# A float32 decoder trunk on one core: another engine for the decays' low halves, other ticks for the decay blocks, another queue for the first transfers

## The chip, the core and the metric

The kernel runs on one core of a Trainium2 chip. The core has a matrix engine (TensorE, here PE), a vector engine (VectorE, here DVE), an engine for activations (ScalarE, here ACT), one for general work (GpSimd, here POOL) and a queue of transfers (SyncE, here SP). Each takes its instructions in order, and they wait for one another through semaphores. The metric is the device time of one execution in microseconds (us), as a median of runs.

## What is computed

One inference step of a two-layer decoder trunk over 336 tokens: 256 of a new prompt, 64 of eight running sequences (8 each), 16 meta tokens. A layer is a half-step SwiGLU block, a mixer, and a second half-step SwiGLU block. The mixer joins gated linear attention (GLA) and a depthwise convolution:

```
proj = x @ w_in
q, k, v, g, a_lr, glu, m_a, m_b = split(proj)
loga = log_sigmoid(a_lr @ w_decay_up + b_decay) / 16
b = cumsum(loga, within a chunk)
scores = mask((q * exp(b)) @ (k * exp(-b)).T)
o = scores @ v + (q * exp(b)) @ S
S = exp(b_last) * S + (k * exp(b_last - b)).T @ v
a, ga = split(glu);  u = a * sigmoid(ga)
c = silu(rmsnorm(depthwise_conv(u, 31 taps)))
merged = sigmoid(m_a) * rmsnorm(o) * silu(g) + sigmoid(m_b) * (c @ w_pw)
h = h + merged @ w_out
```

The decays `loga` and their running sums `b` are what the change is about: they must be ready before the attention can start.

## The kernel before

**Products.** Tokens lie along the free axis, channels along the partitions, eight blocks of 128. All products are made to float32 accuracy from pairs of a shorter type: a value is split into a high half (a cast, `wh`, `xh`, `lah`) and a low half (value minus high half, `wl`, `xl`, `lal`), and each product is three matmuls (`mm3`: high x high, high x low, low x high). One k-step of `mm3` at 336 columns is called a tick.

**Weights.** SP loads 512 KB pieces into four raw buffers (`W.load`), ACT casts each (`wh`, L214), and VectorE (L112, the helper through which all VectorE work is recorded) or POOL (L215) subtracts (`wl`). In the mixer it is POOL for most pieces, the decays' place included; in the SwiGLU blocks it is VectorE. `use` of a piece splits up to three pieces further on and loads up to four more.

**The mixer.** PE goes through three `glu` blocks, then the value blocks with the decays' input, then five more `glu` blocks (`pga`, then `pa`, 8 ticks each). A `glu` block on VectorE is a multiplication of `pga`, after which ACT makes the gate, then one of `pa` and three into `u`. Beside it, work is drawn from a list by ticks (`tasks`, filled from the table `at` in the mixer): decay_z multiplies the low-rank input (`pz`, L463 and on), ACT takes exponential and logarithm, decay_min on VectorE finishes `la` for three groups `g` of tokens at ticks 63, 65, 67, and decay_split (L472 to L474) at ticks 66, 70, 74 casts `lah` on ACT and subtracts `lal`. Then decay_prompt(hd) for the four heads (`pb`): four matmuls each, cumulating `lah` and `lal` of groups 0 and 1, and on ACT three exponentials (`qt`, `kt`, `ku`) and one small one (`dec`, L490). decay_tail(0) and decay_tail(2) do the same for group 2, two heads each (`pbt`). `pb` and `pbt` share one tag of two PSUM buffers, so each waits until the one before the last has been read by ACT.

**Fillers.** VectorE also computes the convolution, 31 taps for each of eight blocks of `u`, a tap being a pair of instructions (`acc`, `acs`, L427 to L430). These pairs are drawn by fill(): the program keeps two estimates of time used, for PE and for VectorE (`clock`; VectorE's is added to by every call through `DVE`), and after each tick adds pairs until VectorE's estimate is 1 us ahead of PE's. After the last tap of a block ACT copies `acc` and `acs` back into `u` (L432 to L435) and squares it (L295). The pairs that are left in the last head are drawn at one place, conv_flush.

**The start.** The first two transfers, the norm columns `vec` and blocks 0 and 1 of `h`, are issued from ACT's queue (L851, L852), beside SP's, which issues the first weight pieces, the rest of `h` and more weights. From `h` and `vec` come `xh` and `xl`; the first weight piece is cast in two parts, and the first matmul follows.

Of the kernel before, what the change touches and what calls it, by code (L numbers as in the profile page):

```python
# [9 lines left out]
F32 = mybir.dt.float32  # L10
# [3 lines left out]
ALU = mybir.AluOpType  # L14
# [38 lines left out]
V_DW = 104  # L53
# [64 lines left out]
def trunk_kernel(ctx, tc, wts, x_in, vecs, consts, cumw, masks, wdecay, cache, state,  # L118
                 y_out, sp_out, ss_out, u_out):
    nc = tc.nc  # L120
    PE, ACT, POOL, SP = nc.tensor, nc.scalar, nc.gpsimd, nc.sync
# [5 lines left out]
    DVE = Clocked(nc.vector, dve_time)  # L127
# [13 lines left out]
    h = cst.tile([128, KB, T], F32, name="h")  # L141
# [3 lines left out]
    vec = cst.tile([128, NV], F32, name="vec")  # L145
# [13 lines left out]
    def vcol(base, l, b, n=KB):  # L159
        return vec[:, base + l * n + b:base + l * n + b + 1]  # L160

    def bank(name, tag="mm", bufs=4):
        return psum.tile([128, 512], F32, tag=tag, name=name, bufs=bufs)
# [155 lines left out]
    def emit_x(b, gcol, norm, n=T, add=True):  # L319
        src = h[:, b, 0:n]  # L320
        ACT.activation(xh[:, b, 0:n], src, AF.Identity, scale=gcol)
        DVE.scalar_tensor_tensor(out=xl[:, b, 0:n], in0=src, scalar=gcol, in1=xh[:, b, 0:n].bitcast(F32),
                                 op0=ALU.mult, op1=ALU.subtract)
        if add:
            norm.add(src, n)
# [43 lines left out]
    def mixer(l, norm, next_block):  # L369
# [8 lines left out]
        lah = mp.tile([128, 3, 512], F32R, tag="wg", name="lah")  # L378
        lal = mp.tile([128, 3, 512], F32R, tag="sb", name="lal")
# [15 lines left out]
        la = {}  # L395
# [75 lines left out]

        def decay_split(g):  # L472
            ACT.copy(lah[:, g], la[g])
            POOL.tensor_tensor(out=lal[:, g], in0=la[g], in1=lah[:, g].bitcast(F32), op=ALU.subtract)  # L474

        def cumulate(out, hd, g):
            hs = slice(hd * DK, (hd + 1) * DK)
            m = cum[:, 0:2 * CHUNK] if g < NCH else cum[:, 2 * CHUNK:N_CUM]
            mm(out, lah[:, g, hs], m, True, False)
            mm(out, lal[:, g, hs], m, False, True)  # L480

        def decay_prompt(hd):
            pb = bank("pb", "aux", 2)
            for g in range(NCH):
                cumulate(pb[:, 2 * g * CHUNK:2 * (g + 1) * CHUNK], hd, g)
            v4 = pb.rearrange("p (g x c) -> p g x c", g=NCH, x=2)
            for dst, x, sign in ((qt, 0, 1.0), (kt, 0, -1.0), (ku, 1, 1.0)):
                ACT.activation(dst[:, hd, 0:SEQ].rearrange("p (g c) -> p g c", g=NCH), v4[:, :, x], AF.Exp,
                               scale=sign / TAU)
            ACT.activation(dec[:, hd, 0:2 * NCH], pb[:, CHUNK - 1::CHUNK], AF.Exp, scale=1.0 / TAU)  # L490

        def decay_tail(h0):
            pb = bank("pbt", "aux", 2)
            for e in range(2):
                cumulate(pb[:, 2 * e * TAIL:2 * (e + 1) * TAIL], h0 + e, NCH)
            v4 = pb[:, 0:4 * TAIL].rearrange("p (h x c) -> p h x c", h=2, x=2)
            hh = slice(h0, h0 + 2)
            for dst, x, sign in ((qt, 0, 1.0), (kt, 0, -1.0), (ku, 1, 1.0)):
                ACT.activation(dst[:, hh, SEQ:T], v4[:, :, x], AF.Exp, scale=sign / TAU)
            ACT.activation(dec[:, hh, 2 * NCH:], v4[:, :, 0, LS - 1:NSAMP:LS], AF.Exp, scale=1.0 / TAU)  # L500
# [65 lines left out]
        at = {0: decay_lr, 20: decay_alr, 50: decay_exp, 54: decay_ln, 118: decay_end}  # L566
        for g in range(3):
            at.update({44 + g: lambda g=g: decay_z(g), 63 + 2 * g: lambda g=g: decay_min(g),
                       66 + 4 * g: lambda g=g: decay_split(g)})
        for hd in range(HEADS):  # L570
            at[82 + 5 * hd] = lambda hd=hd: decay_prompt(hd)
        at.update({103: lambda: decay_tail(0), 109: lambda: decay_tail(2)})
        tasks.extend([at.get(k) for k in range(119)])
        v_proj(1)
        v_proj(2)
# [188 lines left out]
        def head_start(hd):  # L764
            st = hs[hd]
            return {0: lambda: (scores(hd, st), spread_q(hd), mask_ku(hd, st)), 1: lambda: prompt_state(hd, st, 0),
                    2: lambda: prompt_state(hd, st, 1)}
# [22 lines left out]
        at = head_start(0)  # L790
# [57 lines left out]
        mx.close()  # L848

    with tc.manual_schedule():  # L850
        ACT.dma_start(vec[:, :V_DW], vecs[:, :V_DW])  # L851
        ACT.dma_start(h[:, 0:2], x_in[:, 0:2])  # L852
        W.load(1)
        SP.dma_start(h[:, 2:5], x_in[:, 2:5])
        SP.dma_start(h[:, 5:KB], x_in[:, 5:KB])
        W.load(W.RAW - 1)
        DVE.memset(eps, EPS)
        DVE.memset(ones_d, 1.0 / D)
        DVE.memset(ones_v, 1.0 / DV)
        ACT.activation(scratch, eps, AF.Square)  # L860
        DVE.memset(one, 1.0)
        for p in probs:
            DVE.memset(p, 0.0)

        def block_to(base, l, n=T):
            nm = Norm()
            return nm, (lambda b: emit_x(b, vcol(base, l, b), nm, n))

        def side_loads(l):
            ACT.dma_start(u, cache[l])  # L870
            if l == 0:
                SP.dma_start(con, consts)
                SP.dma_start(msk, masks)
                SP.dma_start(vec[:, V_DW:], vecs[:, V_DW:])
                zero = tmp.tile([128, KB], F32, tag="zero", name="zero", bufs=1)
                DVE.memset(zero, 0.0)
                for t in (xh, xl):
                    ACT.copy(t[:, :, T:TP], zero.unsqueeze(2).to_broadcast([128, KB, TP - T]))

        norm = Norm()  # L880
        for b in range(KB):
            emit_x(b, vcol(V_F1, 0, b), norm, add=False)
            if b == 1:
                W.split(1)
        W.split(2)
        for b in range(KB):
            norm.add(h[:, b], eng=DVE)
        for l in range(DEPTH):
            n = TY if l == DEPTH - 1 else T
            nxt, to = block_to(V_MIX, l)  # L890
            ffn(norm, to, ready=KB - 1 if l else 2, aside=lambda: side_loads(l))
            norm = nxt
            nxt, to = block_to(V_F2, l, n)
            mixer(l, norm, to)
            norm = nxt
            if l + 1 < DEPTH:
                nxt, to = block_to(V_F1, l + 1)
            else:
                nxt = Norm()
                to = lambda b, nm=nxt: (nm.add if b < KB - 1 else nm.add_last)(h[:, b, 0:TY], TY)  # L900
            ffn(norm, to, n)
            norm = nxt
        r = norm.rstd(ones_d, TY)
        for b in range(KB):
            DVE.scalar_tensor_tensor(out=h[:, b, 0:TY], in0=h[:, b, 0:TY], scalar=vec[:, V_FIN + b:V_FIN + b + 1],
                                     in1=r[:, 0:TY], op0=ALU.mult, op1=ALU.mult)
            SP.dma_start(y_out[:, b], h[:, b, 0:TY])
# [125 lines left out]
```

## Time and profile before

| | us |
|---|---|
| median of 3 runs | 1633.62 (1631.21 to 1634.97) |
| profiled execution | 1631.83 |
| its span | 1629.7 |
| PE busy | 1598.5 (98%) |
| VectorE busy | 1079.7 (66%) |
| ACT busy | 735.9 (45%) |
| POOL busy | 401.8 (25%) |

The span runs from the program's first instruction to its last; the profiled execution's own time is 2.1 us longer. Busy time is the sum of an engine's instructions; PE's overlap and its weight loads run beside its matmuls. Where an engine has an idle time, the profile names the instruction whose semaphore came last. [...]

### The profile page before, as it was taken

How to read it: one execution, taken by the hardware profiler on the slowest of the kernel's cores; microseconds unless marked ns; L12 is line 12 of the kernel's file. 1: busy time of each engine (PE TensorE's matmuls, PEld its weight loads, DVE VectorE, ACT ScalarE, POOL GpSimd, SP SyncE). 2: the span in 40 equal slices, each digit the busy share in tenths (PEclk: the TensorE clock that was granted, in tenths of full speed). 3: DMA queues.
4: the chain of work that ended last, by engine and by line, in shares of the span. 5: the costliest groups of instructions: out<-in, count | busy, mean ns of one | idle time of the engine just before them, and what ended most of it. 6: DMA issues, size and time to landing. Idle time of an engine off the chain costs nothing.

```text
span 1629.7 us, 26967 instructions
## 1 busy us (share of the span) xinstructions
PE 1598.5 (98%) x10516; PEld 1571.6 (96%) x10516; DVE 1079.7 (66%) x2170; ACT 735.9 (45%) x1153; POOL 401.8 (25%) x290
## 2 busy tenths in 40 slices
PE   7999999999999999999999999999999999999997
PEld 7999999999889999999999999999998799999997
DVE  6656545999986566564456654459999766666633
ACT  5433434673546444333343333346645564443432
POOL 0000005676663300000000000066766632000000
PEclk9999999999999999999999999999999999999999
DMA  5554444555544544444446444444555445444352
GB/s 198 196 171 136 133 144 146 164 158 164 162 163 131 166 131 155 142 131 142 151 139 205 151 132 139 154 131 152 178 174 166 155 141 160 150 157 147 120 169 77
DMA packets 77023, 247.78 MB, mean 152 GB/s; under 512 B 8672, under 2 KB 11360, under 8 KB 76640
## 3 DMA queue, kind: packets, MB, share of 16 engines
q1 hardware_dynamic: 75744, 239.76, 46.1%
q10 hardware_dynamic: 1152, 6.31, 1.1%
q8 instruction: 82, 1.34, 0.3%
q14 instruction: 45, 0.37, 0.1%
HBM read 230.33 MB, written 15.71 MB: 151 GB/s over the span
## 4 chain that ended last, share of the span: by engine, by line
PE 88%; DVE 7%; ACT 1%; DMA 1%; POOL 1%; issue 1%; DVEq 0%; ACTq 0%; POOLq 0%
PE pd L134 20%; PE pg L134 20%; PE pu L134 20%; PE pgate L134 9%; PE po L134 4%; PE pw L134 3%; DVE acc L112 3%; PE pv L134 2%; PE pa L134 2%; PE pga L134 2%; PE pk L134 2%; PE pq L134 2%; DVE acs L112 1%; PE upds L134 1%; PE o L134 1%
## 5 line engine op out<-in xcount | busy, mean ns | idle before, releaser
L112 DVE TENSOR_TENSOR wl<-raw,wh 128x1024 fp32r<-128x1024 f32 (+3 forms) x331 | 361.6, 1109 | 244.2 <-ACT wh L214 243.8
L214 ACT CAST wh<-raw 128x1024 fp32r<-128x1024 f32 (+4 forms) x457 | 427.0, 954 | 60.8 <-issue 26.7
L215 POOL TENSOR_TENSOR wl<-raw,wh 128x1024 fp32r<-128x1024 f32 (+2 forms) x126 | 283.5, 2267 | 144.0 <-ACT wh L214 139.0
L296 POOL TENSOR_TENSOR ssum<-ssum,sq 128x336 f32<-128x336 f32 (+1 forms) x63 | 56.8, 901 | 1025.4 <-ACT sq L295 1025.1
L112 DVE SCALAR_TENSOR_TENSOR acc<-u,vec,acc 128x272 f32<-128x272 f32 (+1 forms) x480 | 234.6, 489 | 0.0
L134 PE MATMUL pg<-xh,wh 128*128 128x336 f32 (+1 forms) x704 | 222.9, 317 | 8.1 <-ACT wh L214 8.1
L134 PE MATMUL pg<-xh,wl 128*128 128x336 f32 (+1 forms) x704 | 222.2, 316 | 0.0
L134 PE MATMUL pu<-xh,wl 128*128 128x336 f32 (+1 forms) x704 | 222.1, 315 | 0.0
L134 PE MATMUL pg<-xl,wh 128*128 128x336 f32 (+1 forms) x704 | 221.9, 315 | 0.0
L134 PE MATMUL pu<-xl,wh 128*128 128x336 f32 (+1 forms) x704 | 221.7, 315 | 0.0
L134 PE MATMUL pu<-xh,wh 128*128 128x336 f32 (+1 forms) x704 | 221.6, 315 | 0.0
L134 PE MATMUL pd<-act_hi,wh 128*128 128x336 f32 (+1 forms) x704 | 221.0, 314 | 0.0
L134 PE MATMUL pd<-act_hi,wl 128*128 128x336 f32 (+1 forms) x704 | 220.4, 313 | 0.0
L134 PE MATMUL pd<-act_lo,wh 128*128 128x336 f32 (+1 forms) x704 | 220.2, 313 | 0.0
L134 PEld LDWEIGHTS pg<-xh,wh 128*128 128x128 f32 x704 | 132.6, 188 | 8.5 <-ACT wh L214 8.1
L352 ACT CAST act_hi<-pu 128x336 fp32r<-128x336 f32 (+1 forms) x88 | 38.4, 437 | 219.1 <-DVE pu L112 219.1
L112 DVE SCALAR_TENSOR_TENSOR acs<-u,vec,acs 128x64 f32<-128x64 f32 x480 | 134.8, 281 | 0.0
L134 PEld LDWEIGHTS pg<-xl,wh 128*128 128x128 f32 x704 | 132.7, 189 | 0.4
L134 PEld LDWEIGHTS pu<-xh,wl 128*128 128x128 f32 x704 | 132.6, 188 | 0.4 <-DVE wl L112 0.4
L134 PEld LDWEIGHTS pg<-xh,wl 128*128 128x128 f32 x704 | 132.7, 189 | 0.2 <-DVE wl L112 0.2
L134 PEld LDWEIGHTS pu<-xh,wh 128*128 128x128 f32 x704 | 132.6, 188 | 0.0
L134 PEld LDWEIGHTS pu<-xl,wh 128*128 128x128 f32 x704 | 132.6, 188 | 0.0
(209 smaller groups left out, 3229.4 us busy)
## 6 DMA issues: line engine op xcount, KB each, us to landing
raw<-in_wts SPq DMA_DIRECT2D x303, 512.0 KB, 3.6
raw<-in_wts SPq DMA_DIRECT2D x64, 384.0 KB, 3.6
raw<-in_wts SPq DMA_DIRECT2D x64, 320.0 KB, 3.0
s<-in_state SPq DMA_DIRECT2D x16, 512.0 KB, 5.6
out_ss<-s SPq DMA_DIRECT2D x16, 512.0 KB, 5.1
raw<-in_wts SPq DMA_DIRECT2D x16, 344.0 KB, 3.3
u<-in_cache ACTq DMA_DIRECT2D x2, 2424.0 KB, 12.0
out_u<-u SPq DMA_DIRECT2D x16, 303.0 KB, 4.5
```

What stands on the lines that cost most here:

```text
L112: return fn(*args, **kw)
L134: PE.matmul(out, a, b, start=start, stop=stop)
L214: ACT.copy(wh[:, cs], raw[:, cs])
L215: eng.tensor_tensor(out=wl[:, cs], in0=raw[:, cs], in1=wh[:, cs].bitcast(F32), op=ALU.subtract)
L296: eng.tensor_tensor(out=self.sum[:, 0:n], in0=self.sum[:, 0:n], in1=sq[:, 0:n], op=ALU.add)
L352: ACT.copy(ah[:, j, 0:n], pu[:, 0:n])
```

## The change

Three edits. decay_split's subtraction moves from POOL to VectorE. decay_prompt is put at ticks 80, 86, 92, 98 instead of 82, 87, 92, 97, and the tails at 104 and 110 instead of 103 and 109. The first two transfers are issued from SP's queue, ahead of the weight pieces, instead of ACT's.

```diff
         def decay_split(g):
             ACT.copy(lah[:, g], la[g])
-            POOL.tensor_tensor(out=lal[:, g], in0=la[g], in1=lah[:, g].bitcast(F32), op=ALU.subtract)
+            DVE.tensor_tensor(out=lal[:, g], in0=la[g], in1=lah[:, g].bitcast(F32), op=ALU.subtract)
...
         for hd in range(HEADS):
-            at[82 + 5 * hd] = lambda hd=hd: decay_prompt(hd)
-        at.update({103: lambda: decay_tail(0), 109: lambda: decay_tail(2)})
+            at[80 + 6 * hd] = lambda hd=hd: decay_prompt(hd)
+        at.update({104: lambda: decay_tail(0), 110: lambda: decay_tail(2)})
...
     with tc.manual_schedule():
-        ACT.dma_start(vec[:, :V_DW], vecs[:, :V_DW])
-        ACT.dma_start(h[:, 0:2], x_in[:, 0:2])
+        SP.dma_start(vec[:, :V_DW], vecs[:, :V_DW])
+        SP.dma_start(h[:, 0:2], x_in[:, 0:2])
         W.load(1)
```

What VectorE is given at the decays of layer 0 changes with the first edit, since a subtraction there counts in the planner's estimate and so takes the place of conv pairs. Before, from the second `la`:

```order
L112 SCALAR_TENSOR_TENSOR la<-pz,la 128x512 x2
L112 SCALAR_TENSOR_TENSOR acc<-u,vec,acc 128x272
L112 SCALAR_TENSOR_TENSOR acs<-u,vec,acs 128x64
L112 TENSOR_TENSOR pga<-pga,rstd 128x336
L112 SCALAR_TENSOR_TENSOR acc<-u,vec,acc 128x272
L112 SCALAR_TENSOR_TENSOR acs<-u,vec,acs 128x64
L112 SCALAR_TENSOR_TENSOR acc<-u,vec,acc 128x272
L112 SCALAR_TENSOR_TENSOR acs<-u,vec,acs 128x64
L112 SCALAR_TENSOR_TENSOR acc<-u,vec,acc 128x272
```

After, from the second `la`:

```order
L112 SCALAR_TENSOR_TENSOR la<-pz,la 128x512
L112 TENSOR_TENSOR lal<-la,lah 128x512
L112 SCALAR_TENSOR_TENSOR la<-pz,la 128x512
L112 TENSOR_TENSOR lal<-la,lah 128x512
L112 TENSOR_TENSOR pga<-pga,rstd 128x336
L112 TENSOR_TENSOR lal<-la,lah 128x512
L112 SCALAR_TENSOR_TENSOR acc<-u,vec,acc 128x272
L112 SCALAR_TENSOR_TENSOR acs<-u,vec,acs 128x64
```

The two `la` are no longer neighbours, the three `lal` stand among them, the third behind `pga`; one conv pair less stands ahead of `pga`. Layer 1 has the same order.

On ACT in layer 0, before, from the gate behind the first two `lah` (`gate` is the sigmoid of a `glu` block, `wh` a weight cast, `qt`, `kt`, `ku`, `dec` the four exponentials of one `pb`, `u` and `sq` a finished conv block):

```order
L546 ACTIVATE gate<-pga 128x336
L214 CAST wh_3385<-raw_3198 128x1024
L473 CAST lah<-la 128x512
L432 COPY u<-acc 128x256
L433 COPY u<-acs 128x64
L435 COPY u<-acc 128x16
L295 ACTIVATE sq<-u 128x336
L214 CAST wh_3442<-raw_3249 128x1024
L488 ACT_TABLE_LOAD
L488 ACTIVATE qt<-pb 128x256
L488 ACTIVATE kt<-pb 128x256
```

After, from the same gate:

```order
L546 ACTIVATE gate<-pga 128x336
L214 CAST wh_3383<-raw_3198 128x1024
L473 CAST lah<-la 128x512
L214 CAST wh_3428<-raw_3249 128x1024
L488 ACT_TABLE_LOAD
L488 ACTIVATE qt<-pb 128x256
L488 ACTIVATE kt<-pb 128x256
L488 ACTIVATE ku<-pb 128x256
L490 ACTIVATE dec<-pb 128x4
L432 COPY u<-acc 128x256
L433 COPY u<-acs 128x64
```

The copies of the finished conv block move from ahead of the first `pb`'s exponentials to behind them, and so ahead of those of the second `pb`. In layer 1 they stay ahead of the first `pb`'s, behind the third `lah` instead of ahead of it.

## Rows read from the trace of the kernel before

**Rows 1.** the page's busy shares by engine over the span: us, share, instructions

```profile
PE 1598.5 (98%) x10516; PEld 1571.6 (96%) x10516; DVE 1079.7 (66%) x2170; ACT 735.9 (45%) x1153; POOL 401.8 (25%) x290
```

**Rows 2.** PE's waits: what was waited for, us in total, times, longest us

```profile
PE pg L134 <- ACT wh L214: 8.1, 1, 8.1
PE pb L134 <- POOL lal L474: 4.5, 4, 1.6
```

**Rows 3.** PE's timeline: start us, us, operation, [idle before <- what ended it]

```profile
334.85 0.39 PE L134 MATMUL pb<-cum,lal 128*128 128x256 f32 x1 [0.73 <-POOL lal L474]
...
1145.79 0.39 PE L134 MATMUL pb<-cum,lal 128*128 128x256 f32 x1 [0.74 <-POOL lal L474]
...
1152.64 0.28 PE L134 MATMUL pb<-cum,lah 128*128 128x256 f32 x1
```

**Rows 4.** two stretches: us, PE busy (count), granted clock, DMA share, GB/s

```profile
335.00:338.00 3.00, 3.00 (x21) 1.00 0.31 124
1146.21:1149.62 3.41, 3.41 (x14) 0.50 0.30 89
```

**Rows 5.** the price on either engine: a tile's row (ns min/median/max), VectorE's timeline

```profile
L474 POOL TENSOR_TENSOR lal<-la,lah x6: 1256/1282/1342, 332.3 to 1148.9; 128x512 fp32r<-128x512 f32 x6
...
8.11 0.69 DVE L112 TENSOR_TENSOR wl<-raw,wh 128x512 fp32r<-128x512 f32 x1
```

**Rows 6.** VectorE beside POOL: their timelines, then two tiles' rows

```profile
455.32 3.52 DVE L112 SCALAR_TENSOR_TENSOR ot<-ot,vec,rstd 128x336 f32<-128x336 f32 x2
...
455.90 2.58 POOL L215 TENSOR_TENSOR wl<-raw,wh 128x1024 fp32r<-128x1024 f32 x1
...
L112 DVE SCALAR_TENSOR_TENSOR ot<-ot,vec,rstd x16: 544/563/2682, 433.7 to 1314.9; 128x336 f32<-128x336 f32 x8, 128x320 f32<-128x320 f32 x8
...
L112 DVE SCALAR_TENSOR_TENSOR u<-u,vec,rstd x16: 533/554/2121, 499.0 to 1311.5; 128x336 f32<-128x336 f32 x8, 128x320 f32<-128x320 f32 x8
```

**Rows 7.** POOL's timeline at the decays of layer 0 and layer 1

```profile
327.55 4.78 POOL L215 TENSOR_TENSOR wl<-raw,wh 128x1024 fp32r<-128x1024 f32 x2 [5.04 <-ACT wh L214]
...
1138.51 4.76 POOL L215 TENSOR_TENSOR wl<-raw,wh 128x1024 fp32r<-128x1024 f32 x2 [5.04 <-ACT wh L214]
```

**Rows 8.** VectorE's timeline at the same places

```profile
329.39 1.28 DVE L112 SCALAR_TENSOR_TENSOR la<-pz,la 128x512 f32<-128x512 f32 x2
...
331.60 0.49 DVE L112 SCALAR_TENSOR_TENSOR acc<-u,vec,acc 128x272 f32<-128x272 f32 x1
...
332.20 0.50 DVE L112 SCALAR_TENSOR_TENSOR acc<-u,vec,acc 128x272 f32<-128x272 f32 x1
...
1140.98 1.28 DVE L112 SCALAR_TENSOR_TENSOR la<-pz,la 128x512 f32<-128x512 f32 x2
```

**Rows 9.** a piece of the chain that ended last: start us, us, what

```profile
1076.35 3.79 PE pga L134 x24
```

**Rows 10.** ACT's timeline at the decays of layer 1

```profile
1145.16 0.38 ACT L432 COPY u<-acc 128x256 f32<-128x256 f32 x1
...
1146.57 1.04 ACT L214 CAST wh<-raw 128x1024 fp32r<-128x1024 f32 x1
1147.63 1.28 ACT L488 ACT_TABLE_LOAD   x1
...
1149.73 0.19 ACT L490 ACTIVATE dec<-pb 128x4 f32<-128x4 f32 x1
```

**Rows 11.** ACT's timeline where layer 0's last head is copied out

```profile
490.28 0.44 ACT L721 COPY ot<-o 128x336 f32<-128x336 f32 x1 [0.76 <-PE o L134]
```

**Rows 12.** the first transfers: ACT's queue, then the chain that ended last

```profile
1.17 0.46 ACTq L852 DMA_DIRECT2D h<-in_x_in  x1
...
1.17 5.27 DMA h<-in_x_in
```

**Rows 13.** two stretches at the start: columns as in rows 4

```profile
1.00:3.00 2.00, 0.00 (x0) 1.00 0.42 103
4.00:5.50 1.50, 0.00 (x0) 1.00 1.03 400
```

## The prediction

> **What bounds the kernel now.** I read the page's busy shares first [rows 1]: TensorE (PE) is busy 98% of 1629.7 us, so an edit can only pay where PE waits. The list of PE's waits is therefore the next view [rows 2]: 8.1 us before the first matmul, and 4.5 us, in four waits, of `pb` on POOL's `lal`; the change aims at both. PE's timeline shows the second of the pair in each layer [rows 3]: 0.73 us at 334.85, 0.74 us at 1145.79; the first take the rest, about 1.5 us each. [...]
>
> All sums are against the profiled execution, 1631.83 us. The median of the runs is 1633.62, and I shift by that difference, 1.8, at the end.
>
> **The subtraction itself.** Six subtractions leave POOL, at 1.28 us each [rows 5]. VectorE (DVE) does the same operation on the same shape, two float32 inputs in SBUF and a 128x512 result, in 0.69 us [rows 5]. That is the price with POOL at rest. With POOL at work the trace shows another [rows 6]: `ot`, median 0.56 us, took up to 2.68, and the place is known. A pair of `ot` began at 455.32 and ended at 458.84, while a POOL weight subtraction ran from 455.90 to 458.48: the second of the pair ends 0.36 us behind POOL. The scaling of `u`, also with two SBUF inputs, reads 2.12 at the most for a median of 0.55. Instructions that take one input from PSUM are not held: while POOL is in weight subtractions [rows 7], the two `la` of 329.39 take 1.28 us together and conv taps 0.60 us a pair [rows 8]. The new `lal` reads `la` and `lah`, both in SBUF. Price: 0.69 us free; held, POOL's end + 0.5 (`ot`'s 0.36, and 0.13 for the longer instruction).
>
> [...]
>
> **Where POOL is at that time.** In both layers it runs two weight subtractions back to back up to the point where it now begins `lal`: 327.55 to 332.33, and 1138.51 to 1143.27 [rows 7]. DVE's order after the change puts `lal` 0 straight behind the second `la`, which is through at 330.00 and 1141.59 (half of the 1.28 us pairs of rows 8). Both fall into POOL's second weight subtraction (in layer 0 by about 0.06 us only). `lal` 0 then ends at 332.33 + 0.5 = 332.83 and 1143.77; `la` 2 (0.55 to 0.6) and `lal` 1 follow, done at 334.04 and 1144.98. Before, POOL's two were ready by 334.8 and 1145.7. The second is 0.75 us earlier; but decay_prompt(0) moves from tick 82 to 80, so PE arrives 6 matmuls x 0.158 = 0.95 us earlier [rows 9] and has these still to do. Net at the same tick: +0.2 us in each layer. The 4.5 us of waiting does not go; it becomes longer.
>
> `lal` 2 waits for `lah` 2 on ACT, behind a gate and a 1.04 us weight cast [rows 10]. That cast releases the next POOL weight subtraction (2.4 us, half of such a pair [rows 7]), which thus starts some 0.5 us before `lal` 2 can. `lal` 2 is held again: done at 338.85 and 1149.8. DVE, in order, has nothing done since `pga`, about 4 us.
>
> **Who waits for that.** Queued behind `lal` 2 on DVE are three conv tap pairs (0.60 us each), the end of a conv block. ACT's copies of the finished block, `u` and its square (about 1.0 us), wait for them, and behind the copies stand the exponentials of `pb`. `pb` and `pbt` take turns in two PSUM buffers, so `pb` 2 needs the exponentials of `pb` 0, `pb` 3 those of `pb` 1, `pbt` 0 those of `pb` 2.
>
> Layer 1: three pairs end at 1151.45, copies and square at 1152.4, cast (1.0) 1153.4, table load (1.3) 1154.75, the four exponentials of `pb` 0 (1.0) at 1155.75; durations from [rows 10] (copies and square: 1145.16 to the next cast at 1146.57, less 0.5 for `lah`). Before, that last one ended at 1149.92 and `pb` 2 ran at 1152.64 without a wait [rows 3]. Both versions have `pb` 2 at tick 92, so this is a comparison at one place: **+3.1 us**. The old clock fall at 1146.21 lies inside and is hidden, if it recurs, by the wait. Without it PE arrives at 1151.3 and waits 4.5 us, with it 2.8. Later steps have time: I find `pb` 3 and `pbt` ready.
>
> Layer 0: here the order has the exponentials of `pb` 0 ahead of the copies, those of `pb` 1 behind. Pairs and the mixing multiplications end at 342.9, copies 344.0, exponentials 345.0; PE reaches `pb` 3 at 343.6 and waits 1.4. Then gate, cast, table load and the exponentials of `pb` 2 end at 350.4, and `pbt` 0, reached at 348.3, waits 2.1. With the +0.2 above: **+3.7 us** (if DVE wins the 0.06 us at the start, 0.55 less). The tails at 104 and 110 move by one tick and cost nothing of their own: the same matmuls behind the same releases, with ACT's exponentials the cover that is gone in layer 0.
>
> **Clock.** Two new long waits come (3 us and 2.8 to 4.5 us). Of the two old ones of 2.2 to 2.3 us, one was followed by a fall [rows 4]. I count one more fall, **+1.7**, with 0 and 3.4 as ends.
>
> **Conv end.** The stall, and taps that the planner moves, leave three pairs more for the flush in the last head, 1.8 us. ACT had 0.76 us of idle time there before the head's output copy [rows 11]; at most 1.0 us a layer shows. I take **+0.5**, ends 0 and 2.
>
> **The first transfers.** `vec` and `h` 0 to 1 go ahead of the first weight piece on SP's queue, issued at 0.74 and 1.15 instead of in parallel on ACT's; behind them every weight piece and the rest of `h` is issued 0.9 us later (two issues of 0.46 [rows 12]). PE's first matmul at 8.13 is the end of a chain: `h` lands at 6.44 [rows 12], and two conversions and the cast follow. DMA moved 103 GB/s to 3.00 us and 400 GB/s from 4.00 us [rows 13]: 0.40 MB in front (52 + 344 KB) has come in soon after 4 us. `h` by the estimate at 5.4, between 4.4 and 6.44, brings the first matmul to about 7.1, 1.0 earlier. But later pieces need the same bytes through a path already at 400 GB/s, so part returns as waits: I take **-0.7**; ends -1.5 and +0.9.
>
> **Sum.** 0.2 + 3.5 in layer 0, 3.1 in layer 1, 1.7 clock, 0.5 conv, -0.7 start = +8.3: 1640.1 on the profiled execution, 1641.9 as a median.
>
> **The rivals.**
> A, works as meant. `lal` takes 0.69 us unheld, PE's `pb` waits go (-4.5), so does the fall (-1.7), start -0.7: -6.9, a median of 1626.7. For it: DVE is twice as quick and has 34% idle over the whole span [rows 1]. Against: [rows 6], and DVE's queue at this place is full (conv fillers). It decides if `lal` 1 is done by about 1141.9, where PE arrives; DVE starts it near 1142.8 even unheld, so not all of the wait can go.
> B, DVE is not held for this instruction. `lal` 1 is done at 331.9 and 1143.4; at `pb` 0 layer 0 gains 2.0 us and layer 1 1.5. But DVE still waits for `lah` 2 and ACT's copies still stand ahead of the exponentials: `pbt` 0 waits 1.75 in layer 0, and `pb` 2 starts near 1152.4 in layer 1, against 1152.64. Sum -0.25 - 0.2 + 0.5 - 0.7 = -0.65: 1633.0, no change.
> C, as the forecast, with falls in both layers and the start lost: 8.3 + 1.7 + 1.6 = +11.6, a median of 1645.2. With no added fall it is 1640.2.
>
> **How the numbers follow.** A measurement of this kernel can tell 0.2%, 3.3 us, from no change. Forecast with C: 0.72 (all its variants lie above 1636.9). B and mixed cases within 0.2%: 0.15. A: 0.13. The range must leave out no more than 0.2. It reaches down to 1631, through B, and up to 1646.5 for C with the conv end's upper value: 0.13 below, some 0.04 above.
>
> **What would show it.** Held: the six `lal` on DVE, three or more at 2.4 to 2.9 us, ending 0.3 to 0.6 us behind a POOL weight subtraction. Unheld: all near 0.7. In PE's waits: `pb` on DVE's `lal` of 3 us a layer, and new waits of `pb` or `pbt` on ACT's exponentials (2.8 to 4.5 us in layer 1; 1.4 and 2.1 in layer 0). ACT waits for DVE's `acc` ahead of the `u` copies. First matmul near 7.1 us. The forecast is wrong if `lal` is unheld, if the exponentials are never waited for, or if the start gives over 3 us.

## The result, and the profile after

The changed kernel takes 1646.47 us as a median of six runs (1644.06 to 1650.13), against 1633.94 (1631.21 to 1640.49) for the kernel before beside it: slower, by a ratio of 1.0088 with a 95% interval of 1.0069 to 1.0107, which is 14.4 us of 1633.6 (11 to 17). A second set, below, gave 1.0080 (1.0057 to 1.0102). The profiled execution is 1644.12 us, its span 1642.3, 12.6 us longer than that of before. The forecast was +8.3, and its range ended at 1646.5, which is +12.9; by their ratios both sets lie above it, the second just so.

PE's waits, in the form of [rows 2] (what was waited for, us in total, times, longest us):

```profile
PE pg L134 <- ACT wh L214: 5.8, 1, 5.8
PE upds L134 <- ACT os L693: 4.9, 2, 3.4
PE pb L134 <- ACT dec L490: 4.3, 1, 4.3
PE pb L134 <- DVE lal L112: 4.3, 4, 1.8
PE upds L134 <- ACT sd L311: 2.4, 2, 1.5
PE pbt L134 <- ACT dec L490: 1.7, 1, 1.7
PE pu L134 <- ACT wh L214: 1.6, 1, 1.6
```

The 4.5 us for POOL's `lal` have become 4.3 us for VectorE's. Two waits are new, of `pb` and `pbt` for the last of ACT's exponentials (`dec`), 6.0 us. The 8.1 us ahead of the first matmul are 5.8, but the second weight piece is now waited for (1.6). The two waits of `upds`, the matmuls that update the running sequences' states `S` where the attention of the four heads is computed (below: the heads), were left alone by the prediction and have grown from 3.7 and 1.9 to 4.9 and 2.4. In the trace of before they read:

```profile
PE upds L134 <- ACT os L693: 3.7, 2, 2.7
PE upds L134 <- ACT sd L311: 1.9, 2, 1.0
```

What happened to the subtraction shows in VectorE's timeline in layer 0 and, behind the dots, POOL's at the same time (they answer to [rows 7, 8]):

```profile
327.48 0.68 DVE L112 SCALAR_TENSOR_TENSOR la<-pz,la 128x512 f32<-128x512 f32 x1
328.07 2.88 DVE L112 TENSOR_TENSOR lal<-la,lah 128x512 fp32r<-128x512 f32 x1
330.87 0.68 DVE L112 SCALAR_TENSOR_TENSOR la<-pz,la 128x512 f32<-128x512 f32 x1
331.48 0.68 DVE L112 TENSOR_TENSOR lal<-la,lah 128x512 fp32r<-128x512 f32 x1
332.07 0.50 DVE L112 TENSOR_TENSOR pga<-pga,rstd 128x336 f32<-128x336 f32 x1
334.55 2.46 DVE L112 TENSOR_TENSOR lal<-la,lah 128x512 fp32r<-128x512 f32 x1 [1.97 <-ACT lah L473]
...
325.65 4.76 POOL L215 TENSOR_TENSOR wl<-raw,wh 128x1024 fp32r<-128x1024 f32 x2 [5.04 <-ACT wh L214]
334.07 5.19 POOL L215 TENSOR_TENSOR wl<-raw,wh 128x1024 fp32r<-128x1024 f32 x2 [3.67 <-ACT wh L214]
```

The same shape takes 2.88, 0.68 and 2.46 us. The 0.68 is the one that begins while POOL is idle (330.41 to 334.07). The first ends at 330.95, 0.54 us behind the end of POOL's pair. The third first waits 1.97 us for its cast and is then held by the next weight subtraction. From the end of `pga` at 332.57 to 337.01 VectorE does nothing else.

Layer 1 shows what hangs on that. ACT's timeline, then PE's, then VectorE's third subtraction (to be read with [rows 10] and [rows 3]):

```profile
1157.11 0.37 ACT L432 COPY u<-acc 128x256 f32<-128x256 f32 x1 [4.11 <-DVE acc L112]
1157.38 0.22 ACT L433 COPY u<-acs 128x64 f32<-128x64 f32 x1
1157.63 0.47 ACT L295 ACTIVATE sq<-u 128x320 f32<-128x320 f32 x1
1158.01 1.03 ACT L214 CAST wh<-raw 128x1024 fp32r<-128x1024 f32 x1
1159.05 1.28 ACT L488 ACT_TABLE_LOAD   x1
...
1161.15 0.19 ACT L490 ACTIVATE dec<-pb 128x4 f32<-128x4 f32 x1
...
1161.40 0.58 PE L134 MATMUL pb<-cum,lah 128*128 128x256 f32 x1 [4.28 <-ACT dec L490]
...
1153.04 2.47 DVE L112 TENSOR_TENSOR lal<-la,lah 128x512 fp32r<-128x512 f32 x1 [1.97 <-ACT lah L473]
```

`lal` 2 is through at 1155.5; three conv pairs follow; ACT, idle for 4.11 us, copies and squares the block, casts a weight, loads a table and takes the exponentials of `pb` 0, the last of which ends at 1161.34; PE, 4.28 us idle, begins `pb` 2 at 1161.40.

The clock that PE was granted (1.00 is full speed), by stretches in the form of [rows 4]:

```profile
333.38:336.79 3.41, 3.41 (x14) 0.50 0.12 47
466.50:473.32 6.82, 6.82 (x25) 0.50 0.25 77
500.63:504.04 3.41, 3.41 (x13) 0.50 0.68 268
1159.40:1166.23 6.83, 4.83 (x18) 0.50 0.37 123
```

A fifth, of 3.41 us, is at 1285.7. Ahead of the end of the program, the kernel before had three, of 3.41 each, at 463.5, 1146.2 and 1303.2. In the one at 1146.2 its `pga` matmuls of 336 columns begin every 0.28 us, ahead of 1142.8, at a clock of 1.00, every 0.155. By these, 1.5 us of 3.41 are lost. The figures below for time lost at the lower clock are half of the stretches' length, an estimate from the clock of 0.50.

### The profile page after: what moved, and what is told of

It reads as the page before. It is cut to its first block, busy times and chain, and to the rows that moved or that the text cites. A ratio compares the mean times of both kernels' runs of the same rounds, so it can differ in the third digit from the quotient of the medians.

```text
span 1642.3 us, 26970 instructions
## 1 busy us (share of the span) xinstructions
PE 1604.7 (98%) x10516; PEld 1576.3 (96%) x10516; DVE 1090.5 (66%) x2176; ACT 736.4 (45%) x1153; POOL 395.2 (24%) x284
## 4 chain that ended last, share of the span: by engine, by line
PE 76%; DVE 18%; ACT 3%; issue 1%; DMA 1%; POOL 0%; SPq 0%; DVEq 0%; ACTq 0%; POOLq 0%
PE pu L134 20%; PE pg L134 20%; PE pd L134 19%; DVE acc L112 8%; PE pgate L134 6%; DVE acs L112 4%; PE po L134 4%; PE pw L134 3%; ACT wh L214 1%; DVE rstd L112 1%; PE upds L134 1%; PE pk L134 1%; PE pq L134 1%; DVE u L112 1%; PE pa L134 1%
## 5 line engine op out<-in xcount | busy, mean ns | idle before, releaser
L134 PE MATMUL pgate<-xh,wh 128*128 128x336 f32 (+1 forms) x384 | 133.6, 348 | 0.1
```

The source lines that it names most:

```text
L134: PE.matmul(out, a, b, start=start, stop=stop)
```

## Experiments

H stands for the theory of the prediction: VectorE is held while POOL runs, and ACT's exponentials come late behind it. Every ratio is of runs beside the kernel before, with a 95% interval; microseconds are the ratio's excess times 1633.6.

**The three edits alone.** The subtraction:

```diff
-            POOL.tensor_tensor(out=lal[:, g], in0=la[g], in1=lah[:, g].bitcast(F32), op=ALU.subtract)
+            DVE.tensor_tensor(out=lal[:, g], in0=la[g], in1=lah[:, g].bitcast(F32), op=ALU.subtract)
```

> The kernel before with VectorE's subtraction alone (old ticks, old queue for the first transfers). Theory H (VectorE is held while POOL runs, and ACT's exponentials come late behind that): lal of 2.4 to 2.9 us where POOL runs, waits of PE for ACT's exponentials at pb or pbt in both layers, and most of the loss of the whole change: +7 to +13 us against before. Rival S (the new ticks bring the loss, the subtraction is a gain): -1 to -5 us, pb waits under 3 us in all.

Measured 1.0057 (1.0042 to 1.0072), +9.3 us; `lal` from 0.67 to 2.89 us. PE's waits at the decays (page of waits):

```profile
PE pb L134 <- ACT dec L490: 5.8, 2, 3.7
...
PE pb L134 <- DVE lal L112: 3.1, 4, 0.9
...
PE pbt L134 <- ACT dec L490: 1.9, 1, 1.9
```

So the loss comes with the subtraction, at the old ticks too. The ticks:

```diff
-            at[82 + 5 * hd] = lambda hd=hd: decay_prompt(hd)
-        at.update({103: lambda: decay_tail(0), 109: lambda: decay_tail(2)})
+            at[80 + 6 * hd] = lambda hd=hd: decay_prompt(hd)
+        at.update({104: lambda: decay_tail(0), 110: lambda: decay_tail(2)})
```

> The kernel before with the new ticks alone (POOL still subtracts). Theory H: PE arrives about 0.95 us earlier at the first pb in each layer, and waits that much longer (pb on POOL's lal 4.5 to about 6.4 us); at the same place behind it nothing is lost, no new waits for ACT: 0 to +2 us, one clock fall of 1.7 at most. Rival S: +6 us or more, with waits of pb or pbt for ACT.

Measured 1.0005 (0.9994 to 1.0016): no difference. The wait for POOL's `lal` grows from 4.5 to 5.8 us, and no wait for ACT comes: PE only waits earlier. The first transfers:

```diff
-        ACT.dma_start(vec[:, :V_DW], vecs[:, :V_DW])
-        ACT.dma_start(h[:, 0:2], x_in[:, 0:2])
+        SP.dma_start(vec[:, :V_DW], vecs[:, :V_DW])
+        SP.dma_start(h[:, 0:2], x_in[:, 0:2])
```

> The kernel before with the first transfers on SP's queue alone. From the changed kernel's trace: first matmul at 5.75 instead of 8.13 us, given back as two waits of the second weight piece by 11 us: -1 to +1 us. Rival: the earlier matmuls are kept, -2.4 us.

Measured 1.0000 (0.9988 to 1.0013). PE's first waits, from that kernel's list:

```profile
PE pg L134 <- ACT wh L214: 5.9, 1, 5.9
...
PE pu L134 <- ACT wh L214: 1.4, 1, 1.4
...
PE pu L134 <- DVE wl L112: 0.3, 1, 0.3
```

The matmuls start 2.2 us earlier; 1.7 us return as waits for the second weight piece, and 20 us into the program nothing is left.

**The hold.** `la` stays in PSUM, written over `pz`, so that `lal` has one input from each memory; order, ticks and cast are those of the change:

```diff
-            DVE.scalar_tensor_tensor(out=la[g], in0=pz[g], scalar=0.0, in1=la[g], op0=ALU.min, op1=ALU.subtract)
+            DVE.scalar_tensor_tensor(out=pz[g], in0=pz[g], scalar=0.0, in1=la[g], op0=ALU.min, op1=ALU.subtract)
...
-            ACT.copy(lah[:, g], la[g])
-            DVE.tensor_tensor(out=lal[:, g], in0=la[g], in1=lah[:, g].bitcast(F32), op=ALU.subtract)
+            ACT.copy(lah[:, g], pz[g])
+            DVE.tensor_tensor(out=lal[:, g], in0=pz[g], in1=lah[:, g].bitcast(F32), op=ALU.subtract)
```

> The changed kernel, with la left in PSUM by the instruction ahead, so that lal has one input in SBUF and one in PSUM; everything else as changed. Theory H: the hold goes, all six lal take about 0.7 us though POOL runs its weight subtractions at the same times; VectorE does not fall behind, pb waits on lal shrink below 3 us in all, the wait for ACT's exponentials in layer 1 shrinks: 8 to 14 us faster than the changed kernel, that is -2 to +4 against before. Rival P (lal is slow on VectorE for another reason, its place in the queue or its inputs' type): lal stays at 2.4 us or more in three or more cases, and the time near +12.

Measured 1.0015 (1.0005 to 1.0025), +2.4 us: some 12 us of the loss gone. The tile's row and the two timelines in layer 0 (VectorE, then POOL):

```profile
L112 DVE TENSOR_TENSOR lal<-pz,lah x6: 678/680/691, 328.3 to 1144.9; 128x512 fp32r<-128x512 f32 x6
...
328.30 0.68 DVE L112 TENSOR_TENSOR lal<-pz,lah 128x512 fp32r<-128x512 f32 x1
...
332.54 0.69 DVE L112 TENSOR_TENSOR lal<-pz,lah 128x512 fp32r<-128x512 f32 x1 [1.94 <-ACT lah L473]
...
325.87 4.75 POOL L215 TENSOR_TENSOR wl<-raw,wh 128x1024 fp32r<-128x1024 f32 x2 [5.05 <-ACT wh L214]
332.10 4.77 POOL L215 TENSOR_TENSOR wl<-raw,wh 128x1024 fp32r<-128x1024 f32 x2 [1.48 <-ACT wh L214]
```

POOL is in its weight subtractions at both places, as in the changed kernel, and the instructions take 0.68 and 0.69 us instead of 2.88 and 2.46. The place in the queue and the operation are unchanged; the memory of one input is the difference (ACT's cast reads that memory too, and takes 0.59 us instead of 0.62). The hold is thus shown, by an instruction that differs in one operand.

**Which of the three.** The third subtraction alone goes back to POOL:

```diff
-            DVE.tensor_tensor(out=lal[:, g], in0=la[g], in1=lah[:, g].bitcast(F32), op=ALU.subtract)
+            eng = DVE if g < 2 else POOL
+            eng.tensor_tensor(out=lal[:, g], in0=la[g], in1=lah[:, g].bitcast(F32), op=ALU.subtract)
```

> The changed kernel, but the third subtraction (group 2, which only the tails read) stays on POOL. Theory H in two parts: VectorE no longer waits for the third cast and POOL's next weight subtraction (about 4 us of VectorE in each layer), so the finished conv block and ACT's exponentials come in time: PE's wait at the third pb of layer 1 (4.3 us) and at the first pbt of layer 0 (1.7) go, or are under 1 us each; the waits for the first two lal stay (about 4.3 us in all). Time +2 to +6 against before, 7 to 11 faster than the changed kernel. Rival (the first lal's hold is what counts): no more than 3 us faster than the changed kernel.

Measured 1.0017 (1.0005 to 1.0029), +2.8 us. The waits of this kernel at the decays:

```profile
PE pb L134 <- DVE lal L112: 4.9, 4, 1.8
...
PE pbt L134 <- ACT dec L491: 0.5, 1, 0.5
```

The wait for the first two stays, 4.9 us, the first still held; the 4.3 at `pb` is gone and `pbt` has 0.5. One subtraction a layer moved back takes away 10 to 12 us, by the second set or the first. Next, the two holds apart, by la in PSUM for some groups only (`lap[g]` is `pz[g]` for these, `la[g]` else; the cast and the subtraction then read `lap[g]`):

```diff
...
+            if g == 2:
+                lap[g] = pz[g]
+            else:
+                lap[g] = la[g]
-            DVE.scalar_tensor_tensor(out=la[g], in0=pz[g], scalar=0.0, in1=la[g], op0=ALU.min, op1=ALU.subtract)
+            DVE.scalar_tensor_tensor(out=lap[g], in0=pz[g], scalar=0.0, in1=la[g], op0=ALU.min, op1=ALU.subtract)
...
```

> The changed kernel with la of group 2 alone in PSUM: the first two subtractions are held as before, the third is not, but still waits on VectorE for its cast (about 2 us). Theory C (the third's place in VectorE's queue costs the most, the cast's wait and the hold in about equal parts): PE's waits for ACT at pb and pbt shrink from 6.0 to 2 to 4 us, the waits for lal stay near 4.3; 3 to 6 us faster than the changed kernel, +6 to +11 against before. Rival F (the first one's hold is what counts): within 2 us of the changed kernel.

> The converse: la of groups 0 and 1 in PSUM, the third held. Theory C: PE's waits for lal go from 4.3 to about 1 us, but PE comes to pb and pbt earlier by that and waits there for ACT's exponentials, which hang on the third: 0 to 3 us faster than the changed kernel, +9 to +14 against before. Rival F: 4 us faster or more, near +6 or under.

(The second has `g < 2` in that line.) Measured 1.0044 (1.0031 to 1.0057), +7.2 us, with the third free and the first held; 1.0056 (1.0043 to 1.0069), +9.1, the other way round. In the first kernel 4.9 us of waits for `lal` and 0.9 for ACT stay; in the second 1.4 and 7.3:

```profile
PE pb L134 <- ACT dec L495: 5.4, 2, 4.3
...
PE pbt L134 <- ACT dec L495: 1.9, 1, 1.9
...
PE pb L134 <- DVE lal L112: 1.4, 3, 0.6
```

Both times lie at the better end of what theory C expected against before. Its waits did not all come: in the first kernel those for ACT are 0.9, not 2 to 4, and the second is 4 to 5 us faster than the changed kernel, not 0 to 3. Freeing the third takes away 6 to 7 us, freeing the first two 4 to 5, and freeing all three 11 to 12 (the smaller figure by the second set of the changed kernel). So both holds count; each of these figures is known to some 4 us, and which hold counts more can't be told.

**The planner's part.** The changed kernel, with the three subtractions kept out of the estimate by which conv pairs are placed:

```diff
-            DVE.tensor_tensor(out=lal[:, g], in0=la[g], in1=lah[:, g].bitcast(F32), op=ALU.subtract)
+            nc.vector.tensor_tensor(out=lal[:, g], in0=la[g], in1=lah[:, g].bitcast(F32), op=ALU.subtract)
```

> The changed kernel, with the three subtractions left out of the planner's estimate, so that the conv pairs stand where they would without them (the subtractions are on VectorE as changed). Theory H: the hold and what follows it make most of the loss; lal stays at 2.4 to 2.9 us where POOL runs, VectorE's idle time ahead of the third stays, and the time is +7 to +13 us against before. Rival Q (the loss comes from conv pairs that the planner moves out of the decays into the heads' stage, where PE's upds waits grew from 3.7 to 7.6 us): +1 to +4 us, with those waits back at about 4 us.

Measured 1.0075 (1.0055 to 1.0095), +12.3 us. The waits of `upds` are back at 3.3 and 1.9 us, as Q has it, but the time is not: the waits for ACT at `pb` and `pbt` grow to 7.5 us. As the main cause Q falls. Side by side with before, in the way of the table below, the heads of this kernel take 2.2 us more (1.7 of it time at the lower clock) and the decays 11.5, where the changed kernel's decays take 8.4: the loss has moved, not gone. The same line with la in PSUM:

> The changed kernel with la in PSUM and the subtractions left out of the planner's estimate. It tells what is left of the loss with the hold gone (+2.4 us with la in PSUM alone). Theory Q for this rest (the conv pairs that the estimate moves): the heads' stage waits are as before (upds about 4 us instead of 6.8) and the time is -3 to +1 against before. Rival (the rest is the exponentials behind the new ticks): PE's waits for ACT at pb and pbt as with la in PSUM alone, 3.9 us, and +2 to +4.

Measured 1.0030 (1.0018 to 1.0042), +4.9 us; `upds` at 4.0 and 1.9, ACT at `pb` and `pbt` 6.4 instead of 3.9. Both theories of the rest missed. In this trace ACT's copies of the finished conv block (335.26 us, in layer 0) stand ahead of the first `pb`'s exponentials (338.58) again, as before the change; with the pairs moved away they follow them (337.17 behind 334.77). In these traces a pair costs PE at either place; the two medians are too near each other to tell which is dearer.

**Ways to both gains.** With la in PSUM, the old ticks:

> The changed kernel with la in PSUM (lal 0.7 us, no hold) and the old ticks. With the hold gone, the old ticks let PE come 0.95 us later to the first pb: its waits for lal under 0.5 us in all, so the 4.5 us of before are gone. If nothing takes their place, -4 us against before. Theory H expects the exponentials to take some of it (ACT's order has a finished conv block ahead of them, and five ticks less room between blocks): PE waits of 2 to 4 us for ACT at pb or pbt, and a time of -3 to +2.

Measured 1.0021 (1.0009 to 1.0034), +3.4: the waits for `lal` are 0.3 us, those for ACT at `pb` and `pbt` 5.6, more than was expected, and the time lies above the range. Then la in PSUM for the first two and the third on POOL, at the new and the old ticks:

```diff
             if g < 2:
                 lap[g] = pz[g]
...
+            eng = DVE if g < 2 else POOL
+            eng.tensor_tensor(out=lal[:, g], in0=lap[g], in1=lah[:, g].bitcast(F32), op=ALU.subtract)
```

> The changed kernel with la of groups 0 and 1 in PSUM (VectorE not held) and the third subtraction on POOL: both causes are taken away. PE's waits for lal about 1 us in all, for ACT's exponentials under 1 us: 4 us of waits less than before. If the theory has all of the loss, -1 to -5 us against before; what is left in the heads' stage (upds waits some 1 to 2 us over those of before) takes the rest. If a cause is missing: 0 to +3.

> The same with the old ticks. PE comes 0.95 us later to the first pb, so it waits under 0.5 us for lal; but five ticks leave ACT less room between blocks. If that room is enough: -2 to -6 us against before, the fastest of all. If not: PE's waits for ACT at pb or pbt of 1 to 3 us and -2 to +2.

Measured 0.9992 (0.9982 to 1.0001) and 0.9999 (0.9989 to 1.0009), medians of 1631.12 and 1632.41 beside 1632.52: the whole loss is gone, no gain is shown. With the old ticks the room is not enough: PE waits 2.5 us for ACT at `pb` and `pbt`, and the time is the one expected for that case. In the first, the waits at the decays:

```profile
PE pb L134 <- DVE lal L112: 1.3, 3, 0.6
...
PE pbt L134 <- ACT dec L496: 0.5, 1, 0.5
```

That is 2.7 us less than before, but `upds` has 5.1 and 2.1 us (3.7 and 1.9 before), and the stretches at the lower clock sum to 13.7 us instead of 10.2 ahead of the end in these two profiles. Over the runs it is the other way: the mean granted clock is 0.9945 and 0.9942 in these two kernels, 0.9928 in the runs of before beside them.

**The size.** The subtraction alone had 1.0057, the whole 1.0088, the other edits nothing of their own. Three runs beside one another, for the second pair of edits with the subtraction:

> VectorE's subtraction with the new ticks, the first transfers as before. If the ticks add to the loss once VectorE is held, this one is as the whole change, +12 to +15 us against before (the subtraction alone took +9.3). If the missing 5 us were scatter between the sets of runs, +8 to +11.

> VectorE's subtraction with the first transfers on SP's queue, old ticks. The transfers alone were worth 0.0: +8 to +11 us against before, as the subtraction alone. If the transfers and the subtraction add up to more than either, +12 or more.

> The changed kernel as it is, beside these two. The first measurement gave 1.0088 with an interval of 1.0069 to 1.0107; the subtraction alone 1.0057. If that gap is real, again 1.0080 or more; if it was scatter, 1.0060 to 1.0075. In its trace, the stretches at the lower clock beside the waits of the heads' stage tell how much of the loss there is clock.

Measured 1.0077 (1.0054 to 1.0101) with the ticks, 1.0080 (1.0056 to 1.0105) with the transfers, 1.0080 (1.0057 to 1.0102) for the whole. By what was expected, all three came out on the side of a real gap. But either edit alone gives as much as both, which no sum of the edits would do, the interval of the subtraction alone reaches into theirs, and about half of the gap lies in the kernel before: its median is 1633.53 beside the subtraction alone and 1631.70 here, against 1642.61 and 1643.5 to 1644.4 for the changed ones. I take it as scatter between sets, which no run settles, with +9 to +14 us for anything that has VectorE's three held subtractions.

The third run brings a second profile of the changed kernel, with a span of 1642.1 us against 1642.3. Its waits, then two rows of PE's timeline:

```profile
PE pb L134 <- DVE lal L112: 5.0, 4, 1.8
PE upds L134 <- ACT os L693: 4.3, 2, 3.4
PE pb L134 <- ACT dec L490: 3.9, 2, 2.8
...
PE upds L134 <- ACT sd L311: 1.9, 2, 1.0
PE pbt L134 <- ACT dec L490: 1.9, 1, 1.9
...
343.85 0.38 PE L134 MATMUL pb<-cum,lah 128*128 128x256 f32 x1 [1.14 <-ACT dec L490]
...
1161.00 0.58 PE L134 MATMUL pb<-cum,lah 128*128 128x256 f32 x1 [2.76 <-ACT dec L490]
```

The waits are of the same kind, but the stretches at the lower clock ahead of the end sum to 13.7 us, against 23.9 in the first profile of the same kernel.

## Why the prediction was right and wrong

To set terms against terms I put the start of the same matmul in the two profiled executions side by side, and took how the distance grew from stage to stage. A matmul of 325.0 us in the trace of before starts 1.93 us earlier in that of after; one of 352 us, 1.72 later; and so on. The last column does the same with the second profile of the changed kernel.

| stretch (us of before) | forecast | distance grew by | second profile |
|---|---|---|---|
| start, to 20 | -0.7 | +0.3 | 0.0 |
| first SwiGLU block, 20 to 176 | 0 | -2.2 | -2.2 |
| decays of layer 0, 325 to 352 | +3.7 | +3.7 | +3.9 |
| heads of layer 0, 390 to 500 | +0.5 (both layers) | +5.9 | +3.1 |
| decays of layer 1, 1140 to 1165 | +3.1 | +4.8 | +4.8 |
| heads of layer 1, 1255 to 1340 | (above) | +1.2 | +2.1 |
| clock, wherever | +1.7 | within these | within these |
| all other stretches | 0 | -1.1 | +0.7 |
| sum | +8.3 | +12.6 | +12.4 |

**The subtraction: right.** The price of a held `lal`, POOL's end + 0.5, was 330.41 + 0.54 and, in layer 1, 1148.88 + 0.56 (POOL's pair from 1144.12 takes 4.76 us, the `lal` begun at 1147.19 takes 2.25). All six behaved as forecast, four held and two free. In layer 0 the first came just behind the start of the second of POOL's pair (328.07, where half of the pair's 4.76 us is through at 328.03); the forecast had 0.06 us to spare there, so that this one would be held was a near thing, worth 0.55 us by the forecast.

**Who waits: right, in size too.** Layer 1's wait at `pb` 2 was forecast at 4.5 us without a fall of the clock ahead of it and 2.8 with one. The first profile has no fall there and 4.28, the second a fall at 1150.7 and 2.76; from 1140 us to this matmul the distance grew by 2.5 and 3.2, with +3.1 forecast. Layer 0's wait at `pbt` 0 was forecast at 2.1 and is 1.73 and 1.85. The forecast 1.4 at `pb` 3 did not come in the first trace, where the clock had fallen at 333.38 and PE was, by the estimate above, 1.7 us later; in the second, without that fall, it is 1.14. The net in layer 0 comes out the same.

**Rival B** describes what la in PSUM makes of the kernel. Its wait at `pbt` is there, 1.4 us where B put 1.75, but B came to -0.65 and +2.4 (0.8 to 4.1) was measured. B used the same term for the heads as the forecast.

**The ticks: right as nothing.** I had them move a wait, not make one; alone they measured +0.8 (-1 to +2.6).

**The step that failed is the term "conv end".** It was taken as 0.5 us with ends of 0 and 2: three conv pairs more a layer for the flush, mostly covered by ACT's idle time ahead of one copy in the last head [rows 11]. The heads took 7.1 us in the first profile and 5.2 in the second; without the time at the lower clock that is 3.7 and 5.2. The count was not far off: VectorE's timeline has 94 conv pairs instead of 89 in the heads of layer 0, three of the five behind 475 us as forecast, and 33 instead of 30 in those of layer 1. The cover was wrong. ACT's idle time in [rows 11] ends with PE's `o` and is no slack of VectorE's, where the pairs stand among state updates and gates: `upds` waits 3.37 us instead of 2.70 at 466, 1.46 instead of 0.95 at 499.6, and 0.34 at 420.9 where nothing waited. That is 1.5 us, which the `upds` row of PE's waits before would have put on the list. With the pairs left in place there are 89 and 30 again, the `upds` waits are back at 3.3 and 1.9 us, and the heads of layer 0 take 0.2 us more than before beside the clock. So in layer 0 the pairs are the cause, as far as one trace can show it. Part of the rest stands in no wait for VectorE or ACT (in the second profile PE waits 1.5 us more for the states' transfers, `pso`), and its cause stays open.

**The clock term was too sure, and too small by what the runs have in the mean.** Stretches at a granted clock of 0.50 ahead of the end went from 10.2 us to 23.9 in the first profile; 2.0 us of that lie in PE's wait at `pb` 2. Half of the difference of the rest, 5.8 us, is lost by the estimate above, 3.4 of it in the heads of layer 0, and I had one fall of 1.7, at the decays, with an upper end of 3.4. No run shows the 1.7 itself: it is half of 3.41, where the starts of the matmuls give 1.5. In the second profile the same sum gives 1.7, as forecast, and its span is as long: one trace can't size this term. Over all runs the mean granted clock is 0.9900 in twelve runs of the changed kernel and 0.9927 in 88 of the kernel before, by estimate a difference of 4.5 us at full speed, of which some lies inside waits and costs nothing. The falls also come where I hadn't counted any: behind the waits of `upds` (at 466.50 and 500.63 in the first profile), which the kernel before has too (463.5, behind 2.70 us).

**The range.** Its upper end was C with the conv end at 2 us (by the working 1646.7, where 1646.5 was written). It failed by the same two terms.

**The start: right in kind.** The matmul began even earlier than I took it (5.75, not 7.1), and gave it all back. The term of -0.7 assumed that some would be kept.

**Rival A** would have needed `lal` 1 by the time PE arrives. With the hold gone and the third on POOL the waits at the decays fall to 1.8 us, and the time still doesn't fall clear of before's: in that kernel's profile the decays take 4.3 us less than before and the heads 5.2 more, 3.4 of it at the lower clock.

**What stays open.** Why the time does not fall with the waits in the last two kernels. Their two traces show longer `upds` waits and more time at the lower clock, but the clock of all their runs is higher than before's, so the clock is not the answer for the medians. And the falls differ between executions, so their share in the medians can't be told from single profiles.

## What to carry to other kernels

Ahead of a move of an element-wise step from POOL to VectorE, lay POOL's timeline beside the place where it will stand: here, with both inputs in SBUF, the subtraction took 2.25 to 2.88 us beside POOL's weight subtractions, its first in each layer ending 0.54 and 0.56 us behind POOL's pair, and 0.68 with POOL idle. With one input left in PSUM it took 0.68 to 0.69 us beside them. The third, which nothing soon needs (only the tails read it), was better left on POOL than put into the queue that feeds ACT (1.0017 instead of 1.0088 or 1.0080). And where a planner's estimate counts the moved step, follow the fillers that it pushes out, to the stage where they land (here 94 conv pairs instead of 89 in the heads of layer 0).

## What the runs showed of the hardware

The hold depends on where `la`, one of the two inputs, lies: 2.88 and 2.46 us with it in SBUF, 0.68 and 0.69 us with it in PSUM, beside the same POOL instructions. POOL pays too: its pair beside the third subtraction took 5.19 us, and 4.77 with `la` in PSUM.

The first SwiGLU block runs at two speeds in these profiles, though the granted clock is 1.00 in both. From 30 to 170 us the kernel before issued 902 matmuls in its profiled execution, the kernel after 915, with the same instructions in both (columns as in [rows 4]; the kernel before, then after):

```profile
30.00:170.00 140.00, 140.00 (x902) 1.00 0.50 165
...
30.00:170.00 140.00, 140.00 (x915) 1.00 0.51 166
```

The profile with the third subtraction's la in PSUM has 902 as well, that with the third on POOL and two in PSUM 915, and so have those of the ticks alone and of the subtraction alone; no edit goes with it, and its cause is not known. A comparison of single traces can be off by two us for this alone: it is the -2.2 of the table, and may be why the two traces differ by 12.6 us and the medians by 14.4.

After the same wait the time at the lower clock differs: with the ticks alone, `upds` waits 2.71 us, as before (2.70), and the stretch from 461.29 is 6.83 us long instead of 3.41:

```profile
461.29:468.12 6.83, 6.47 (x23) 0.50 0.31 93
...
463.55:466.96 3.41, 3.41 (x14) 0.50 0.27 65
```

The first row is of the kernel with the ticks alone, the second of the kernel before. The changed kernel does the same: behind a wait of 3.37 us the stretch is 6.82 us long in its first profile and 3.41 in its second. In the five profiles of kernels in which VectorE has three held subtractions and the planner counts them, the stretches ahead of the end sum to 13.7 to 27.3 us, so a term for them is better given as a range of one to five more than as one fall.
